# New tables of units, turns and product order in a two-layer trunk with seven-product weight pairs

## The chip, the cores and the metric

The kernel runs on one core of a Trainium2 chip. The metric is the device time of one execution in microseconds, the median of several runs. The profile is of one execution; its times are in microseconds from the start of its span.

## The reference

The reference is a trunk of two transformer layers in float32 on a sequence of 256 tokens with D = 2048, 16 heads of 128 and an MLP of 8192. What matters here is its chain of matrix products:

```python
u = rms_norm(h, a_norm_g[l]);  proj = u @ a_w_in[l]          # 2048 x 6160
o = forgetting_attention(q, k, v, logf)
h = h + o.reshape(B, S, D) @ a_w_out[l]
h = h + sq_relu_mlp(h, mlp_norm_g[0], mlp_w1[0], mlp_w2[0])  # a = relu(u @ w1); (a * a) @ w2
kv = rms_norm(h, kv_norm_g) @ kv_w
q = rms_norm(h, b_norm_g[l]) @ b_w_q[l]
o = chunked_relbias_attention(q, k_sh, v_sh, b_rel[l])
h = h + o.reshape(B, S, D) @ b_w_out[l]
h = h + sq_relu_mlp(h, mlp_norm_g[1], mlp_w1[1], mlp_w2[1])
```

All weights are used once and together are about 0.5 GB, so they stream through the core while TensorE works.

## The kernel before

**A unit.** A weight panel of 512 columns is read in units of two k-tiles, 128 x 1024 float32 numbers, 512 KB. `load` issues a unit's transfer on SP's queue into one of four buffers (`raw`). `issue` splits a unit in two: ScalarE copies it to `hi` (L256), VectorE computes `lo = raw - hi` (L257). TensorE then runs three passes (L519, L521, L523): activations' `hi` by `hi`, activations' `lo` by `hi`, activations' `hi` by `lo`. A whole unit is twelve matmuls of 512 columns. `top_up` keeps two split units ready ahead of the one that TensorE works on, and three units loaded beyond these. `hi` and `lo` have three buffers each.

**A pair.** In the MLPs and in the query projection two neighbouring panels, a and b, are a `Pair`. A part of its k-tiles goes through a seven-product scheme on 2 x 2 blocks (two halves of these k-tiles by two panels), with two blocks of tokens as the third side. Blocks are named 11, 12, 21, 22. Seven "made" forms are multiplied, in the order 11, T3, T2, T1, 21, T4, 22, where T3 = 22 + 12, T2 = T3 + 11, T1 = 12 + 11 and T4 = 21 + T2. In the MLPs all pairs but the first have eight k-tiles in the scheme (`deep`): a block is 128 x 2048, 1 MB, and a form is multiplied in two halves f and h of six matmuls each. The other eight k-tiles of each panel are its own units, a4 to a7 and b4 to b7. (The first pair and the query's two have four k-tiles in the scheme and own units from 2 on.)

**Where made forms come from.** `bring` loads blocks on SP's queue (L860) into four rooms of one buffer each, so the transfer waits until the room's last reader is done. The rooms change hands from pair to pair: block 12 goes where the pair before had 11, 22 where it had 12, 11 where it had 21, 21 where it had 22. T3 and T2 are sums on VectorE (L876) in a room of their own; T2 is made when T3 has been split. T1 and T4 are made by a transfer with addition (`put`, L882), issued from POOL: T1 adds block 11 onto the tile of 12, T4 adds block 21 onto the tile of T2, and that is issued when T2 has been split.

**The order of work.** `plan_mlp` writes one list of all items for a layer's MLP. W1 and W2 alternate: W2 of chunk c and W1 of chunk c + 1, each with q = 0 and 1. The orders of a cycle are called "deep0" (W2, q = 0), "ahead0" (W1, q = 0), "deep1" (W2, q = 1), "ahead1" (W1, q = 1). `Pair.plan` puts the first four forms in front, with b5, b6, b7 of the pair before between them, and then follows `ORDERS`, where each F stands for the next made form:

```python
plan = made[0] + rest[:1] + made[1] + rest[1:2] + made[2] + rest[2:] + made[3]
```

**When blocks are fetched.** After each own unit `prepare` looks at how many own units remain until the next pair starts, and issues what that pair's row of `UNITS` asks for at this count: loads of 12, 22, 21 and 11, the sum T3 (in two halves, the second a unit later) and the transfer for T1, in this order of the six numbers. A larger number is earlier. W1E belongs to the first pair, W1I1 to the second, W1F and W1S to W1 with q = 0 and 1, W2F, W2S and W2L to W2 with q = 0, with q = 1 and to the last one, QF and QS to the query's pairs.

**Small work.** Everything else is cut into steps in the queue `fill`; one step is run after each own unit and after each form of a deep pair. `TURNS` has the steps of a hidden panel (first row group: chunk 0, second: the later chunks; four panels each): the first number is the step of its transposing transfers (a `hop` of 16 transfers, half on SP and half on POOL, where the second number is -1, else a way through memory that needs a second step), then follow ReLU, the square's `hi`, the square, its `lo`, and for the first two panels the sums that the scheme needs of the activations. `LONG` and `SHORT` are the same for the panels of the residual stream.

**Queues.** VectorE, ScalarE, TensorE and SP execute in the written order (`keep_order`). SP issues unit loads, block loads, turns and half of the hops; an issue that waits for its room holds all that are behind it.

Of the kernel before, what the change touches and what calls it, by code (L numbers as in the profile page):

```python
# [26 lines left out]
NEG = -1.0e30  # L27
UN = 1024
AHEAD = 2
ORDERS = {  # L30
# [7 lines left out]
}  # L38
UNITS = {
    "W1I1": (9, 7, 6, 5, 4, 1),  # L40
    "W1F": (6, 5, 1, 4, 4, 1),
    "W1S": (6, 5, 2, 4, 4, 3),
    "W2F": (7, 5, 1, 5, 4, 3),
    "W2S": (8, 8, 3, 4, 3, 2),
    "W2L": (6, 6, 1, 3, 3, 1),
    "QF": (5, 4, 1, 4, 3, 3),
    "QS": (7, 5, 1, 4, 3, 2),
}
TURNS = (
    ((1, -1, 4, 5, 6, 6, 6, 9, 9),  # L50
     (0, -1, 3, 5, 7, 7, 8, 9, 9),
     (1, -1, 5, 7, 7, 7),
     (1, -1, 3, 4, 5, 5)),
    ((0, -1, 4, 14, 14, 14, 14, 19, 19),
     (0, 3, 7, 10, 10, 13, 16, 18, 19),
     (1, -1, 4, 6, 7, 7),
     (0, -1, 4, 5, 5, 5)),
)
EARLY = 3
# [3 lines left out]
DEEP = 2 * UN  # L63
WIDE1 = (1, 2, 3, 4, 5, 6, 7)
# [15 lines left out]
def trunk(ctx: ExitStack, tc: tile.TileContext, xT, xr, gs, hg, bf, wgate, w_in, w_oa, w1a, w1fa, w1sa, w2fa, w2sa,  # L80
# [68 lines left out]
    class Pair:  # L149
# [12 lines left out]
        def plan(self, rest):  # L162
            made = [self.items(f"f{i} h{i}" if self.wide else f"f{i}") for i in range(7)]
            own = ORDERS[self.order].split()
            plan = made[0] + rest[:1] + made[1] + rest[1:2] + made[2] + rest[2:] + made[3]
            n = 4
            for i in own:
                if i == "F":
                    plan += made[n]
                    n += 1  # L170
                else:
                    plan += self.items(i)
            return plan, self.items("b5 b6 b7")

    def plan_mlp(w1, w1f, w1s, w2f, w2s, tail, more=None):
        pairs = []

        def add(w, wf, ws, i, wides, order, when, cols=WIDE):
            j = wides.index(i) if i in wides else i - sum(1 for k in wides if k < i)
            names = ("11", "12", "21", "22")  # L180
            if i in wides:
                m = 8 - cols // 512
                src = [[None] * (8 - m) + [ws[m * (2 * j + q) + u] for u in range(m)] for q in range(2)]
                big = {k: wf[4 * j + m] for m, k in enumerate(names)}
            else:
                src = [[w[16 * j + 8 * q + u] for u in range(8)] for q in range(2)]
                big = {k: src[int(k[1]) - 1][int(k[0]) - 1] for k in names}
            pairs.append(Pair(big, src, order, len(pairs) % 2 == 0, when, cols if i in wides else UN))

        rooms = {"12": "v0", "22": "k0", "11": "k1", "21": "v1"}  # L190
        seq = [(0, 0, 0), (0, 0, 1)]
        for c in range(NCH):
            seq += [(1, c, 0)] + [(0, c + 1, 0)] * (c + 1 < NCH) + [(1, c, 1)] + [(0, c + 1, 1)] * (c + 1 < NCH)
        for m, (second, c, q) in enumerate(seq):
            i = 2 * c + q
            if second:
                add(None, w2f, w2s, i, WIDE2, "deep%d" % q, UNITS["W2L" if i == 7 else "W2S" if q else "W2F"], DEEP)
            else:
                add(w1, w1f, w1s, i, WIDE1, "ahead%d" % q if i else "early", (25, 20, 9, 15, 10, 8) if not i else UNITS["W1I1" if i == 1 else "W1S" if q else "W1F"], DEEP)
            pairs[-1].at = second, c, q  # L200
        if more is not None:
            for q in range(2):
                add(more, None, None, q, (), "" if q else "query", UNITS["QS" if q else "QF"])
                pairs[-1].at = 1, NCH, q
        plan, rest = [], [(tail, 0, u) for u in range(KT // UA - 3, KT // UA)]
        for p in pairs:
            p.rooms = rooms
            if p.adds:
                rooms = {"12": rooms["11"], "22": rooms["12"], "11": rooms["21"], "21": rooms["22"]}
            mine, rest = p.plan(rest)  # L210
            plan += mine
        plan += rest
        units.extend(Form(p, i, q == 3) if q > 1 else p.src[q][i] for p, q, i in plan)
        return plan

# [3 lines left out]
    queue(w_oa, n_out)  # L219
    tail_a = Tail(w_oa, n_out - 5)  # L220
    plan_a = plan_mlp(w1a, w1fa, w1sa, w2fa, w2sa, tail_a, w_qb)
    for i in range(w_kv.shape[0]):
        units.append(w_kv[i])
    queue(w_ob, n_out)
    tail_b = Tail(w_ob, n_out - 5)
    plan_b = plan_mlp(w1b, w1fb, w1sb, w2fb, w2sb, tail_b)
    ready = deque()

# [38 lines left out]
    def half_next():  # L267
        u = raws[0][0] if raws else units[0]
        return isinstance(u, Form) and u.half and not u.pair.deep

    def top_up(ahead=AHEAD, early=EARLY):
        while (units or raws) and sum(1 for r in ready if not r[2]) <= ahead and not (half_next() and any(r[2] for r in ready)):
            issue()
        while units and sum(1 for r in raws if r[1]) < early:
            load()

    def fetch(ahead=AHEAD, early=EARLY):
        top_up(ahead, early)
        return ready.popleft()[:2]
# [58 lines left out]
    def room(tag, name, dtype=F32):  # L338
        return qkv.tile([P, DEEP], dtype, name=name, tag=tag, bufs=1)
# [69 lines left out]
        return query[0][:, i * UN : i * UN + UN]  # L409


    LONG = ((0, 0, 1, 3, 10, 11, 12, 13, 13), (0, 1, 2, 4, 8, 9), (0, 1, 1, 3, 5, 6), (0, 0, 1, 3, 5, 6))
    SHORT = ((3, 1, 2, 3, 6, 7, 9, 9, 10), (4, 2, 3, 5, 10, 11, 13, 14, 22), (1, 2, 3, 4, 9, 10), (0, 0, 1, 2, 4, 5))

    def next_x(n, r2, stats, which, into, kept=None, fs=None, then=None, thirds=True):
        add_h = residual(n, r2)
        zt, way = [], []
        fs = fs if n < 1 + thirds else None
        at = (LONG if kept is not None else SHORT)[n]

# [41 lines left out]
    class RowStats:  # L462
# [4 lines left out]
        def add(self, b, n):  # L467
            t = wk.tile([P, 512], F32, name="sqr", tag="wk")
            S.activation(t, h[b][:, n * 512 : (n + 1) * 512], AF.Square, accum_out=self.ss[:, b * NG + n : b * NG + n + 1])
# [57 lines left out]
    def products(ps, hi, lo, x, u, halves=False, fast=None, apart=False):  # L527
        kw = {"skip_group_check": True} if fast else {}

        def item(j, b):  # L530
            k = u * UA + j if fast is None or u > 1 else 2 * j + u
            return ps[b], [x[k][:, i, b * P : (b + 1) * P] for i in range(2)], j, k == 0 and not fast, k == KT - 1

        J, B = range(UA), range(NB)
        if apart:
            groups = [[(j, b) for b in B] for j in J]
        elif halves:
            groups = [[(j, b) for j in J] for b in B]
        else:
            groups = [[(j, b) for b in B for j in J]]  # L540
        for g in groups:
            items = [item(*i) for i in g]
            for c in HALVES if halves and g is groups[-1] else (slice(0, 512),):
                passes(items, hi, lo, c, **kw)
# [14 lines left out]
    def panels(x, evacs, before=None, after=None, which=(None, None), tail=None):  # L559
        ps = [acc_pair(i) for i in which[: len(evacs)]]  # L560
        for u in range(KT // UA - (3 if tail else 0)):
            if before:
                before(u)
            for q, evac in enumerate(evacs):
                hi, lo = fetch(min(u // 2, AHEAD), 2) if before else fetch()
                products(ps[q], hi, lo, x, u, not units and not ready, apart=u < 2 if before else len(evacs) == 2 and (u, q) == (KT // UA - 1, 0))
# [196 lines left out]
    early = room("bias", "early")  # L763
# [120 lines left out]
    def prepare(p, d):  # L884
        if p.deep and d == p.units[4] - 1:
            make(p, "T3", 1)
        for name, at in zip(("12", "22", "21", "11", "T3", "T1"), p.units):
            if d == at and p.deep and name == "T3":
                make(p, "T3", 0)
            elif d == at:  # L890
                (bring if name[0] != "T" else put if p.adds and name == "T1" else make)(p, name)

    def mlp(plan, x, Sx, st, last, more=None):
        base = turns[0]
        hids = [[] for _ in range(NCH)]
# [57 lines left out]
        for i, (p, q, u) in enumerate(plan):  # L953
# [5 lines left out]
            if q > 1:  # L959
# [6 lines left out]
                if q == 2 + p.wide:  # L966
                    if not p.deep:
                        top_up(AHEAD - 1)
                    if u == 1:
# [170 lines left out]
```

## Time and profile before

| | us |
|---|---|
| median of 3 runs | 2092.68 (2088.75 to 2097.32) |
| the profiled execution | 2090.07 |
| its span | 2088.3 |
| TensorE busy | 2068.8 |
| VectorE busy | 1710.9 |
| ScalarE busy | 1313.2 |
| POOL busy | 224.7 |

The granted TensorE clock is 0.998 on average. The transfers move 543 MB, 260 GB/s on average. Lines of the profile name the engine, the kernel's line, the operation, the tile written and the tiles read; a bracket after it, or the part behind a bar, is the engine's idle time ahead of it and what ended that. A line of waits has the waiting instruction, whom it waited for, the total in us, the number of times and the longest. A line of a stretch (from:to) has its length, the busy time of PE, PE's weight loads, VectorE, ScalarE and POOL with the number of instructions, then TensorE's granted clock, the share of the transfer engines and GB/s. A line of transfers ends with their count, size and median time from issue to landing in us.

### The profile page before, as it was taken

The numbers are of one execution on the slowest core, as the hardware profiler recorded it, in microseconds if no ns is written. First come the engines' busy times: TensorE is split into PE (matmuls) and PEld (weight loads), VectorE is DVE, ScalarE is ACT, GpSimd is POOL, SyncE is SP. The second block draws the span as 40 slices with busy tenths as digits, with TensorE's granted clock in tenths as the row PEclk, the third lists the DMA queues.
The fourth block names the chain that finished last, engine by engine and source line by source line (L and its number), as shares of the span: only waits on it lengthen the run. The fifth ranks groups of instructions, "written<-read, shape, count | busy, mean of one in ns | idle before, by whom it ended". The sixth has DMA issues, their size and how long they took to land.

```text
span 2088.3 us, 26874 instructions
## 1 busy us (share of the span) xinstructions
PE 2068.8 (99%) x9140; PEld 1703.1 (82%) x9140; DVE 1710.9 (82%) x1974; ACT 1313.2 (63%) x1587; POOL 224.7 (11%) x339
## 2 busy tenths in 40 slices
PE   9999999999999999999999999999999999999999
PEld 7888888877888887888878888888788888888887
DVE  5767666898898898888988677768988988988986
ACT  6544444676676676576777445456766676766764
POOL 1111000021101102101011000000211111011020
PEclk9999999999999999999999999999999999999999
DMA  8777778787988898898978767787889889888875
GB/s 286 248 250 245 227 255 264 270 250 243 293 268 268 267 292 244 270 280 265 283 241 269 236 225 237 235 268 272 275 268 295 241 268 291 266 269 267 291 241 182
DMA packets 170682, 543.08 MB, mean 260 GB/s; under 512 B 40480, under 2 KB 68528, under 8 KB 147504
## 3 DMA queue, kind: packets, MB, share of 16 engines
q1 hardware_dynamic: 153008, 463.16, 62.9%
q0 software_dynamic: 17248, 77.64, 18.7%
q8 instruction: 72, 1.18, 0.2%
q10 hardware_dynamic: 288, 0.57, 0.1%
q14 instruction: 66, 0.54, 0.1%
HBM read 501.39 MB, written 26.24 MB: 253 GB/s over the span
## 4 chain that ended last, share of the span: by engine, by line
PE 76%; issue 10%; DMA 10%; DVE 3%; ACT 1%; POOL 0%; SPq 0%; ACTq 0%; DVEq 0%; POOLq 0%
PE acc L523 21%; PE acc L519 20%; PE acc L521 20%; PE s L523 4%; PE s L519 4%; PE s L521 4%; DVE lo L257 2%; DMA w<-in_w2fa 1%; DMA wT<-in_w2fa 1%; DMA turn<-z 1%; DMA wT<-in_w2fb 1%; ACT hi L256 1%; DMA w<-in_w2fb 1%; DMA w<-in_w1fb 1%; DMA raw<-in_w2sa 1%
## 5 line engine op out<-in xcount | busy, mean ns | idle before, releaser
L256 ACT ACTIVATE hi<-raw 128x1024 fp32r<-128x1024 f32 (+1 forms) x514 | 540.4, 1054 | 344.6 <-PE acc L521 257.6
L257 DVE TENSOR_TENSOR lo<-raw,hi 128x1024 fp32r<-128x1024 f32 (+1 forms) x514 | 618.6, 1212 | 165.0 <-ACT hi L256 150.0
L519 PE MATMUL acc<-hi,act 128*128 128x512 f32 x2076 | 580.7, 395 | 9.8 <-ACT hi L256 8.4
L523 PE MATMUL acc<-lo,act 128*128 128x512 f32 x2076 | 570.9, 390 | 1.0 <-DVE lo L257 0.6
L521 PE MATMUL acc<-hi,act 128*128 128x512 f32 x2076 | 570.4, 390 | 0.2
L519 PEld LDWEIGHTS acc<-hi,act 128*128 128x128 f32 x2076 | 387.6, 188 | 92.3 <-ACT hi L256 11.7
L523 PEld LDWEIGHTS acc<-lo,act 128*128 128x128 f32 x2076 | 389.0, 188 | 86.6 <-DVE lo L257 6.2
L521 PEld LDWEIGHTS acc<-hi,act 128*128 128x128 f32 x2076 | 390.2, 188 | 83.4 <-DVE act L350 1.5
L256 ACT ACTIVATE hi<-w 128x1024 fp32r<-128x1024 f32 x258 | 270.7, 1057 | 109.0 <-PE acc L521 68.2
L257 DVE TENSOR_TENSOR lo<-w,hi 128x1024 fp32r<-128x1024 f32 x258 | 310.1, 1219 | 18.9 <-ACT hi L256 17.7
L257 DVE TENSOR_TENSOR lo<-wT,hi 128x1024 fp32r<-128x1024 f32 x184 | 222.2, 1221 | 74.9 <-ACT hi L256 73.6
L256 ACT ACTIVATE hi<-wT 128x1024 fp32r<-128x1024 f32 x184 | 192.9, 1058 | 110.6 <-PE acc L521 35.6
L395 POOL DMA_DIRECT2D q<-z x208 | 105.6, 547 | 266.5 <-DVE z L369 127.2
L519 PE MATMUL s<-hi,act 128*128 128x512 f32 x358 | 98.5, 390 | 0.5 <-DVE s L976 0.5
L523 PE MATMUL s<-lo,act 128*128 128x512 f32 x358 | 98.5, 390 | 0.0
L521 PE MATMUL s<-hi,act 128*128 128x512 f32 x358 | 98.2, 389 | 0.0
L876 DVE TENSOR_TENSOR wT<-w,w 128x1024 f32<-128x1024 f32 x62 | 75.4, 1217 | 7.9 <-DMA w<-in_w1fb 2.7
L519 PEld LDWEIGHTS s<-hi,act 128*128 128x128 f32 x358 | 67.1, 188 | 14.8 <-issue 0.9
L523 PEld LDWEIGHTS s<-lo,act 128*128 128x128 f32 x358 | 67.0, 188 | 14.5 <-DVE lo L257 0.8
L521 PEld LDWEIGHTS s<-hi,act 128*128 128x128 f32 x358 | 67.2, 188 | 14.0
L876 DVE TENSOR_TENSOR wT<-wT,w 128x1024 f32<-128x1024 f32 x62 | 76.0, 1225 | 2.1
L605 POOL TENSOR_TENSOR ss<-ss,mhalf 128x4 f32<-128x4 f32 x32 | 43.3, 1360 | 273.0 <-DVE ss L604 272.8
(181 smaller groups left out, 1820.5 us busy)
## 6 DMA issues: line engine op xcount, KB each, us to landing
raw<-in_w_in SPq DMA_DIRECT2D x95, 512.0 KB, 4.3
w<-in_w2fa SPq DMA_DIRECT2D x32, 1024.0 KB, 6.7
raw<-in_w2sa SPq DMA_DIRECT2D x64, 512.0 KB, 6.5
raw<-in_w_kv SPq DMA_DIRECT2D x64, 512.0 KB, 4.5
w<-in_w2fb SPq DMA_DIRECT2D x32, 1024.0 KB, 6.5
raw<-in_w2sb SPq DMA_DIRECT2D x64, 512.0 KB, 6.6
w<-in_w1fa SPq DMA_DIRECT2D x28, 1024.0 KB, 7.7
raw<-in_w1sa SPq DMA_DIRECT2D x56, 512.0 KB, 7.1
```

The source lines that it names most:

```text
L256: S.activation(hi[:, c], raw[:, c], AF.Copy)
L257: V.tensor_tensor(lo[:, c], raw[:, c], hi[:, c].bitcast(F32), op=ALU.subtract)
L395: (G if i % 2 else SY).dma_start(dst[32 * j : 32 * j + 32, i * n : (i + 1) * n], z[32 * i : 32 * i + 32, j * n : (j + 1) * n])
L519: TE.matmul(ps[:, cols], xh, cut(hi, j), start=first, stop=False, **kw)
L521: TE.matmul(ps[:, cols], xl, cut(hi, j), start=False, stop=False, **kw)
L523: TE.matmul(ps[:, cols], xh, cut(lo, j), start=False, stop=last, **kw)
L605: G.tensor_tensor(rn, vv, mhalf, op=ALU.pow)
L876: V.tensor_tensor(d, a, b, op=ALU.add)
```

## The change

The change touches tables alone, and one new table `LAST`, by which an order may multiply its last three made forms in another sequence. In "deep0" that sequence is 21, 22, T4, and all three stand right behind a4. In "deep1" the last form moves behind a5. In "ahead1" T4 moves ahead of a5. The rows of `UNITS`, `TURNS`, `LONG` and `SHORT` get other numbers; the row of the first pair moves from the code into the table as W1E.

```diff
+LAST = {"deep0": (4, 6, 5)}
 ORDERS = {
...
-    "deep0": "a4 F F b4 a5 F a6 a7",
-    "deep1": "a4 F b4 F F a5 a6 a7",
+    "deep0": "a4 F F F b4 a5 a6 a7",
+    "deep1": "a4 F b4 F a5 F a6 a7",
     "ahead0": "F a4 F a5 a6 a7 F b4",
-    "ahead1": "a4 F a5 F a6 a7 F b4",
+    "ahead1": "a4 F F a5 a6 a7 F b4",
 }
 UNITS = {
-    "W1I1": (9, 7, 6, 5, 4, 1),
-    "W1F": (6, 5, 1, 4, 4, 1),
-    "W1S": (6, 5, 2, 4, 4, 3),
-    "W2F": (7, 5, 1, 5, 4, 3),
-    "W2S": (8, 8, 3, 4, 3, 2),
-    "W2L": (6, 6, 1, 3, 3, 1),
-    "QF": (5, 4, 1, 4, 3, 3),
-    "QS": (7, 5, 1, 4, 3, 2),
+    "W1E": (25, 20, 9, 14, 11, 10),
+    "W1I1": (9, 7, 5, 6, 4, 1),
+    "W1F": (7, 5, 1, 5, 4, 3),
+    "W1S": (8, 6, 4, 5, 4, 1),
+    "W2F": (6, 5, 1, 5, 4, 3),
+    "W2S": (7, 7, 4, 5, 3, 1),
+    "W2L": (7, 5, 1, 5, 4, 2),
+    "QF": (7, 6, 1, 3, 2, 1),
+    "QS": (7, 5, 1, 5, 2, 2),
 }
 TURNS = (
-    ((1, -1, 4, 5, 6, 6, 6, 9, 9),
-     (0, -1, 3, 5, 7, 7, 8, 9, 9),
-     (1, -1, 5, 7, 7, 7),
+    ((0, -1, 4, 5, 6, 6, 6, 7, 9),
+     (0, -1, 3, 6, 7, 7, 7, 8, 8),
+     (0, -1, 4, 7, 7, 7),
      (1, -1, 3, 4, 5, 5)),
-    ((0, -1, 4, 14, 14, 14, 14, 19, 19),
-     (0, 3, 7, 10, 10, 13, 16, 18, 19),
-     (1, -1, 4, 6, 7, 7),
+    ((1, -1, 5, 14, 14, 14, 15, 20, 20),
+     (0, 2, 8, 10, 10, 14, 18, 20, 22),
+     (0, -1, 5, 6, 7, 7),
      (0, -1, 4, 5, 5, 5)),
 )
...
             own = ORDERS[self.order].split()
+            last = LAST.get(self.order, (4, 5, 6))
...
-                    plan += made[n]
+                    plan += made[last[n - 4]]
...
-    ... "early", (25, 20, 9, 15, 10, 8) if not i else UNITS[...]
+    ... "early", UNITS["W1E" if not i else ...]
...
-    LONG = ((0, 0, 1, 3, 10, 11, 12, 13, 13), (0, 1, 2, 4, 8, 9), (0, 1, 1, 3, 5, 6), (0, 0, 1, 3, 5, 6))
-    SHORT = ((3, 1, 2, 3, 6, 7, 9, 9, 10), (4, 2, 3, 5, 10, 11, 13, 14, 22), (1, 2, 3, 4, 9, 10), (0, 0, 1, 2, 4, 5))
+    LONG = ((1, 0, 2, 4, 9, 11, 11, 13, 14), (0, 1, 2, 4, 7, 9), (0, 1, 1, 3, 5, 5), (0, 0, 1, 1, 4, 5))
+    SHORT = ((4, 1, 2, 3, 6, 6, 9, 9, 10), (4, 2, 3, 5, 10, 11, 13, 15, 23), (1, 2, 2, 3, 9, 9), (1, 0, 1, 2, 4, 5))
```

More of the change, by code (lines that the diff above doesn't have):

```diff
@@ L198, in plan_mlp @@
             else:
-                add(w1, w1f, w1s, i, WIDE1, "ahead%d" % q if i else "early", (25, 20, 9, 15, 10, 8) if not i else UNITS["W1I1" if i == 1 else "W1S" if q else "W1F"], DEEP)
+                add(w1, w1f, w1s, i, WIDE1, "ahead%d" % q if i else "early", UNITS["W1E" if not i else "W1I1" if i == 1 else "W1S" if q else "W1F"], DEEP)
             pairs[-1].at = second, c, q
```

## The prediction

> **What bounds the kernel now.** I read the totals of the page first, then TensorE's own waits.
>
> ```profile
> span 2088.3 us, 26874 instructions
> PE 2068.8 (99%) x9140; PEld 1703.1 (82%) x9140; DVE 1710.9 (82%) x1974; ACT 1313.2 (63%) x1587; POOL 224.7 (11%) x339
> ...
> PE acc L519 <- ACT hi L256: 8.4, 7, 2.6
> PE s L523 <- DVE lo L257: 2.0, 4, 1.0
> ```
>
> TensorE is the bound: 2088.3 - 2068.8 = 19.5 us of the span are not its own. The change adds and removes no matmul, so it can only move waits. In the timeline, a unit and a form at full pace, in the first pair of W1 that has the wide form, look like this:
>
> ```profile
> 442.84 1.07 PE L519 MATMUL acc<-hi,act 128*128 128x512 f32 x4
> 443.75 1.07 PE L521 MATMUL acc<-hi,act 128*128 128x512 f32 x4
> ...
> 445.56 0.62 PE L519 MATMUL acc<-hi,act 128*128 128x512 f32 x2
> ```
>
> Four matmuls take 443.75 - 442.84 = 0.91 us, 0.2275 us each, and a unit of twelve takes 445.56 - 442.84 = 2.72 us. A form is six and six, so one step of a plan, unit or form, is 2.72 us. The busy time of PE hides short waits (ends are modelled), so I count starts. In stretches of 8 us:
>
> ```profile
> 480.00:488.00 8.00, 6.13 (x28) 4.73 (x26) 4.40 (x5) 1.98 (x3) 3.94 (x8) 1.00 0.79 205
> 488.00:496.00 8.00, 7.54 (x26) 6.06 (x27) 6.89 (x6) 7.38 (x9) 0.03 (x1) 0.79 0.87 294
> 648.00:656.00 8.00, 7.28 (x31) 5.37 (x29) 5.87 (x8) 3.57 (x5) 3.95 (x8) 1.00 0.75 192
> 816.00:824.00 8.00, 6.63 (x29) 4.85 (x28) 5.29 (x6) 3.87 (x4) 2.77 (x6) 1.00 0.73 203
> 980.00:988.00 8.00, 8.00 (x37) 6.64 (x36) 7.69 (x8) 4.92 (x6) 3.89 (x8) 1.00 0.86 281
> 1519.00:1527.00 8.00, 8.00 (x37) 6.52 (x36) 6.91 (x7) 4.80 (x6) 3.97 (x8) 1.00 0.84 239
> 1684.00:1692.00 8.00, 7.94 (x34) 5.96 (x33) 6.60 (x7) 5.00 (x6) 3.00 (x7) 1.00 0.81 256
> 1848.00:1856.00 8.00, 7.45 (x31) 5.50 (x31) 6.09 (x7) 3.86 (x4) 3.87 (x8) 1.00 0.70 199
> 2013.00:2021.00 8.00, 7.94 (x35) 6.08 (x35) 6.87 (x8) 4.64 (x5) 3.40 (x7) 1.00 0.80 269
> ```
>
> The first bracket counts matmuls. An undisturbed stretch has 37, as the rows at 980 and 1519 show. These nine rows lie around the eight places where a "deep0" pair (W2, q = 0) comes to its form T4. They lack 9, 11, 6, 8, 0, 0, 3, 6 and 2 matmuls, 45 in all, and 45 x 0.2275 = 10.2 us. That is nearly half of all that TensorE loses in the MLPs: sixteen further stretches that I looked at lack 55 (12.5 us), these six among them:
>
> ```profile
> 445.00:453.00 8.00, 7.23 (x31) 5.34 (x30) 6.63 (x8) 6.73 (x8) 0.00 (x0) 1.00 0.96 386
> 573.00:581.00 8.00, 7.78 (x35) 6.12 (x34) 6.36 (x7) 5.05 (x6) 0.00 (x0) 1.00 1.04 333
> 738.00:746.00 8.00, 7.02 (x31) 5.51 (x30) 6.41 (x6) 5.82 (x6) 0.00 (x0) 1.00 0.96 301
> 1076.00:1084.00 8.00, 6.77 (x29) 4.96 (x28) 4.06 (x5) 4.07 (x7) 0.68 (x1) 1.00 0.98 358
> ...
> 1754.00:1762.00 8.00, 7.64 (x33) 5.69 (x32) 4.68 (x5) 6.44 (x8) 0.92 (x1) 1.00 0.86 299
> 1937.00:1945.00 8.00, 7.93 (x35) 6.27 (x34) 5.91 (x6) 5.58 (x6) 0.00 (x0) 1.00 0.95 309
> ```
>
> **What ends the wait in deep0.** The chain, the timeline and the table of waits agree:
>
> ```profile
> 473.85 13.40 DMA wT<-in_w2fa
> ...
> 487.36 2.00 ACT L256 ACTIVATE hi<-wT 128x1024 fp32r<-128x1024 f32 x2 [6.02 <-DMA wT<-in_w2fa]
> 488.46 0.99 PE L519 MATMUL acc<-hi,act 128*128 128x512 f32 x2 [2.34 <-ACT hi L256]
> ...
> ACT hi L256 <- DMA wT<-in_w2fa: 19.7, 6, 6.0
> ```
>
> T4 is made by a transfer that adds block 21 onto T2. It is issued as soon as T2 has been split, takes 13.40 us here, and then ScalarE copies, VectorE subtracts and TensorE starts. Between T2 and T4 in deep0 lie b7, T1, a4 and 21. That is about one step too little.
>
> The row at 488 also shows a granted clock of 0.79 after this one wait; the two stretches around it lack 20 matmuls, 4.6 us, though the idle time is 2.34 us. [...]
>
> **Part by part.**
>
> *deep0: "a4 F F F b4" with made order 21, 22, T4.* T4 comes one step (2.72 us) later after T2, and 22, a raw block that is there long before, fills in. Seven of the eight waits are shorter than 2.72 us; the first is about as long. All but some 0.4 us of the 10.2 go: -9.8 us. The room of T4 comes free a step later; it is the next pair's T3, which is made at b4, and b4 itself moves behind T4, so nothing queues there.
>
> *ahead1: "a4 F F a5" instead of "a4 F a5 F".* The same thing the other way round: T4 comes 2.72 us earlier. How much room it had:
>
> ```profile
> 442.88 2.01 ACT L256 ACTIVATE hi<-wT 128x1024 fp32r<-128x1024 f32 x2 [2.41 <-DMA wT<-in_w1fa]
> ...
> 611.77 2.15 ACT L256 ACTIVATE hi<-wT 128x1024 fp32r<-128x1024 f32 x2 [1.02 <-DMA wT<-in_w1fa]
> 613.12 1.07 PE L519 MATMUL acc<-hi,act 128*128 128x512 f32 x4
> ...
> 1481.98 2.01 ACT L256 ACTIVATE hi<-wT 128x1024 fp32r<-128x1024 f32 x2 [2.56 <-PE acc L523]
> 1484.51 0.62 PE L519 MATMUL acc<-hi,act 128*128 128x512 f32 x2
> ...
> wT<-in_w2fa POOLq DMA_DIRECT2D x8, 1024.0 KB, 10.6
> wT<-in_w1fa POOLq DMA_DIRECT2D x7, 1024.0 KB, 9.3
> ```
>
> A copy is half of the row at 442.88, about 1.05 us. In the pair at 611.77 it is done at 612.8, and T4's matmuls would be wanted at 613.12 (where a5 stands now): just in time, with VectorE's part, about 1.2 us more against 0.91 us of matmuls, a tenth too late. At 442.88 the copy ends at 443.9, wanted at 442.84: 1.1 us late, with VectorE's part 1.4. At 1481.98 it ends at 1483.0, wanted at 1484.51 - 2.72 = 1481.79: 1.2 late, 1.6 with the rest. The six others are like the one at 611.77 or a little looser: 0.5 us together. Sum +3.5 us. Bounds: nothing, if the transfers of the first pair meet less traffic; 10.2 us, if these T4 behave as deep0's do now. I take 3.5, because the median landing, 9.3, is that of W1, not the 10.6 of W2.
>
> *deep1: form 22 moves behind a5, and W1S loads 22 at 6 instead of 5.* At 738, 573 and 1937 deep1 waits in front of 22:
>
> ```profile
> 741.95 1.23 DVE L876 TENSOR_TENSOR wT<-w,w 128x1024 f32<-128x1024 f32 x1 [0.82 <-DMA w<-in_w1fa]
> 743.10 2.35 DVE L257 TENSOR_TENSOR lo<-w,hi 128x1024 fp32r<-128x1024 f32 x2
> ```
>
> The sum T3 of the next pair waits for its load, and the subtraction for 22 stands behind it on VectorE. The load comes a unit earlier and 22 a unit later: 6 + 2 + 2 matmuls, -2.3 us. The first load of that row, 12, goes from 6 to 8, but it needs the room of block 11, which is only free when T2 is made: it holds SP's queue for that time. Units are loaded three ahead, 8.2 us, which covers it: 0.
>
> *Hidden turns: ReLU at step 5 instead of 4 in the later chunks, sums spread to 20 and 22.* The wait at 1754 (4 matmuls) stands behind a ReLU whose turned tile is still landing:
>
> ```profile
> ACT q L899 <- DMA q<-z: 5.4, 4, 2.0
> ```
>
> One step later takes it out: -0.9 us.
>
> *T1 of deep1 (W2S, 2 to 1).* It may now stand behind the eight turn transfers on POOL:
>
> ```profile
> 648.96 3.55 POOL L395 DMA_DIRECT2D q<-z  x7 [5.41 <-DVE z L369]
> ...
> w<-in_w2fa POOLq DMA_DIRECT2D x8, 1024.0 KB, 9.3
> ```
>
> Eight by 0.51 are 4.1 us, 9.3 to land, 1.05 to copy: 14.5 us, and from b4 to T1 lie six steps, 16.3 us. The steps hide it; without a margin of 1.8 us it would cost its excess six times.
>
> *All else* (W1E, W1I1, W2F, W2L, QF, QS, LONG, SHORT) has one answer, no term of its own: loads asked for a unit earlier or later mostly wait for their room, not for the table. The wait at 1076 is a turned tile of the last panel on its way, which LONG doesn't shorten. But some sixty numbers are new, and each can put two bursts together. The other sixteen places cost 12.5 us with the old numbers; 3.2 of it are counted as gone above. New ones are bounded by nothing and by another 12.5; I take about a quarter, +3.5 us.
>
> **Sum:** -9.8 + 3.5 - 2.3 - 0.9 + 3.5 = -6.0 us. The profiled execution took 2090.07 us, 1.8 more than its span, so it would take 2084.1. It lies 2.6 below the median of 2092.68; from the median, 2086.7 us, 0.29% less.
>
> **Rivals.**
>
> *All waits go.* ahead1's T4 is in time everywhere and the new tables make no new waits, even take 1 us off the rest: -9.8 - 2.3 - 0.9 - 1.0 = -14.0, 2078.7 us. For it: every edit that I can price, except ahead1, loosens a wait that the trace shows. Against it: the rows at 442.88 and 1481.98 say that two T4 are late.
>
> *The wait only moves from deep0 to ahead1.* T4 in ahead1 then costs the full 10.2: -13.0 + 10.2 + 3.5 = +0.7, 2093.4 us. For it: after the change ahead1 has the order, and the load of 12 at 6, which deep0 has now. Against it: 12 waits for T2 in either place, and W1's landings are shorter. [...]
>
> *Slower: SP's queue stands.* In deep1 the load of 21 now comes at b4 and waits until the split of 22, which has moved behind a5. Behind it stand all unit loads of b5 and on, and the turns' transfers. From b4 to 22 are three steps, 8.2 us, and the units loaded ahead cover as much. If the hold outlasts them, TensorE waits for the excess, and with a slow clock for more. At 3.5 us in each of the six deep1 pairs before a W1: -9.5 + 3.5 + 21.0 = +15, 2107.7 us. It decides against the change from an excess of 1.0 us (six times that eat the 6.0), and passes 0.5% from 2.8 us. Against it: SP runs ahead of TensorE, so the hold begins and ends early.
>
> **How the numbers follow.** Forecast 0.52, all waits go 0.18, moves 0.17, slower 0.13. About 0.5% (10.5 us) is what a measurement of this kernel can tell from no change: 2082.2 and 2103.1 are the marks. Faster: the 0.18 and the lower edge of the forecast, 0.07, together 0.25. Slower: nearly all of the 0.13 and a little of the moved wait, 0.13. Same: 0.62. The range runs from 2077, below the case in which all goes, to 2102: it leaves out the slower case and the extremes of the others. Its upper part takes in ahead1's bound of 10.2 and new waits of up to 12.5 us together: -13.0 + 10.2 + 12.5 = +9.7, 2102.4.
>
> **What would show it.** Right: in deep0 T4's copy no longer ends a wait on "DMA wT<-in_w2f", counts of 36 or 37 there; in ahead1 a first copy that waits for "DMA wT<-in_w1f", with 1 to 2 us of PE idle in the first wide W1 pair of each layer and next to nothing later; no VectorE wait for "w<-in_w1f" ahead of T3 in deep1. Wrong: PE idle over 1 us in the later ahead1 pairs, waits on "raw<-in_w2s" in deep1, or a second stretch with a granted clock below 1.

## The result, and the profile after

| | before | after |
|---|---|---|
| median of 6 runs, us | 2090.91 (2088.75 to 2097.32) | 2077.85 (2074.23 to 2080.62) |
| the profiled execution, us | 2090.07 | 2078.09 |
| its span, us | 2088.3 | 2076.2 |
| TensorE's waits in the pairs, us | 23.0 | 13.4 |

The ratio is 0.9932, with an interval of 0.9916 to 0.9949. The forecast was 0.29% less, and it became 0.68%, more than twice as much. The time lies just inside the lower end of the range (2077 to 2102), beside the rival "all waits go" (2078.7 us).

The last row of the table is used throughout. It is worked out from the starts of the 8838 matmuls of the three passes: whatever the distance from one start to the next has beyond 0.232 us is summed over the pairs of the MLPs and of the query projection. It counts waits and slow matmuls alike, and does not suffer from modelled ends.

The page of the kernel after, its totals and the head of its chain:

```profile
span 2076.2 us, 26893 instructions
...
PE 2062.0 (99%) x9140; PEld 1702.9 (82%) x9140; DVE 1712.5 (82%) x1974; ACT 1313.2 (63%) x1587; POOL 222.9 (11%) x339
...
PE 95%; DMA 3%; ACT 1%; DVE 1%; issue 0%; POOL 0%; ACTq 0%; DVEq 0%; SPq 0%; POOLq 0%
```

The other engines' busy times are within 2 us of those of before, as it must be where nothing but the order changes. PE's busy time is 6.8 us shorter; I read that as short waits and slow matmuls that the busy time had hidden. The span minus it is 14.2 us, where it was 19.5.

The stretches around deep0's T4, in the kernel after (columns as in the prediction; the first bracket counts TensorE's matmuls, 37 is a full stretch):

```profile
478.00:486.00 8.00, 8.00 (x37) 6.64 (x36) 7.15 (x9) 4.87 (x6) 3.97 (x8) 1.00 0.67 174
648.00:656.00 8.00, 8.00 (x37) 6.60 (x36) 7.46 (x8) 6.05 (x7) 1.22 (x3) 1.00 0.79 277
812.00:820.00 8.00, 8.00 (x37) 6.60 (x36) 7.46 (x7) 6.58 (x7) 0.54 (x2) 1.00 0.78 280
1518.00:1526.00 8.00, 7.75 (x35) 6.10 (x34) 4.99 (x6) 6.12 (x7) 0.00 (x0) 1.00 0.83 328
1840.00:1848.00 8.00, 8.00 (x37) 6.64 (x36) 7.49 (x7) 6.06 (x7) 1.81 (x4) 1.00 0.70 237
2003.00:2011.00 8.00, 8.00 (x37) 6.64 (x36) 7.60 (x8) 6.06 (x6) 2.02 (x5) 1.00 0.71 242
```

Five of the six rows are full, where the nine rows of before lacked 45; the granted clock is 1.00 in all. The row at 1518 lacks two, not at T4 but at b4, the unit behind it: there the ReLU of a hidden turn waits 1.62 us on ScalarE for its turned tile, and b4's copy stands behind it. T4 of deep0 no longer stops TensorE. What still does, in the table of waits of the kernel after (waiting instruction, whom it waited for, total in us, number, longest):

```profile
PE acc L522 <- ACT hi L259: 3.4, 3, 1.3
PE s L522 <- ACT hi L259: 2.6, 2, 2.4
...
ACT hi L259 <- DMA wT<-in_w1fa: 9.3, 5, 3.1
...
ACT hi L259 <- DMA raw<-in_w2sa: 6.7, 4, 4.8
```

All lines are three higher than before (L256 is L259, L519 is L522, L860 is L863). The first row was 8.4 us in seven waits. The transfer that TensorE is kept waiting for at T4 is now W1's, in ahead1, no longer W2's. ScalarE still waits for W2's in four places, 5.7 us together, which costs TensorE nothing. And there is a wait that before did not have: a plain unit of W2 (`raw<-in_w2sa`), which TensorE meets as the 2.4 of the second row.

By place, the 23.0 us went as follows:

| place | before | after |
|---|---|---|
| T4 in deep0 and b4 right behind it (8 pairs; after, all of it at b4) | 9.4 | 0.7 |
| form 22 in deep1 | 2.05 | 0 |
| T4 in ahead1, first wide W1 pair of each layer | 0 | 3.3 |
| first wide pairs: a6, T3, 11 | 4.5 | 1.6 |
| T2 in deep1, second layer | 0.9 | 0 |
| last W2 pairs | 1.2 | 0 |
| query pairs | 3.15 | 2.9 |
| own unit b5 in deep1 | 0 | 2.65 |
| the rest | 1.8 | 2.2 |

Of the 12.1 us between the spans 1.9 lie ahead of the first item of the pairs: it starts at 375.6 us in the trace of before and at 373.7 after. That is not put down to the change, although `SHORT` and W1E do move a little ahead of that item. In the seventeen traces of this study it starts either between 373.1 and 374.1 or between 375.1 and 375.7, with either tables: the kernel after showed 373.7, 375.6 and 373.7, and the old `SHORT` and the old loads of W1E showed 375.6 in the kernel before and 373.9 in the kernel with deep0's order alone.

### The profile page after: what moved, and what is told of

It reads as the page before. It is cut to its first block, busy times and chain, and to the rows that moved or that the text cites. A ratio compares the mean times of both kernels' runs of the same rounds, so it can differ in the third digit from the quotient of the medians.

```text
span 2076.2 us, 26893 instructions
## 1 busy us (share of the span) xinstructions
PE 2062.0 (99%) x9140; PEld 1702.9 (82%) x9140; DVE 1712.5 (82%) x1974; ACT 1313.2 (63%) x1587; POOL 222.9 (11%) x339
## 4 chain that ended last, share of the span: by engine, by line
PE 95%; DMA 3%; ACT 1%; DVE 1%; issue 0%; POOL 0%; ACTq 0%; DVEq 0%; SPq 0%; POOLq 0%
PE acc L526 25%; PE acc L524 25%; PE acc L522 25%; PE s L522 6%; PE s L524 6%; PE s L526 6%; PE s L666 1%; PE po L696 1%; DMA raw<-in_w2sa 1%; DMA wT<-in_w1fa 1%; DMA raw<-in_w2sb 1%; DMA raw<-in_w1b 0%; DMA query<-turn 0%; ACT hi L259 0%; PE po L697 0%; PE s L665 0%
## 5 line engine op out<-in xcount | busy, mean ns | idle before, releaser
L259 ACT ACTIVATE hi<-raw 128x1024 fp32r<-128x1024 f32 (+1 forms) x514 | 540.4, 1054 | 341.4 <-PE acc L524 251.4
L522 PE MATMUL acc<-hi,act 128*128 128x512 f32 x2076 | 578.3, 394 | 5.4 <-ACT hi L259 3.4
L522 PEld LDWEIGHTS acc<-hi,act 128*128 128x128 f32 x2076 | 387.4, 188 | 85.4 <-ACT hi L259 4.5
L259 ACT ACTIVATE hi<-w 128x1024 fp32r<-128x1024 f32 x258 | 271.1, 1058 | 120.9 <-PE acc L524 105.5
L259 ACT ACTIVATE hi<-wT 128x1024 fp32r<-128x1024 f32 x184 | 193.3, 1059 | 88.6 <-PE acc L524 34.6
L522 PE MATMUL s<-hi,act 128*128 128x512 f32 x358 | 98.8, 391 | 3.1 <-ACT hi L259 2.6
L522 PEld LDWEIGHTS s<-hi,act 128*128 128x128 f32 x358 | 66.8, 188 | 18.4 <-ACT hi L259 3.9
```

Source lines behind the costliest of these rows:

```text
L259: S.activation(hi[:, c], raw[:, c], AF.Copy)
L522: TE.matmul(ps[:, cols], xh, cut(hi, j), start=first, stop=False, **kw)
```

## The experiments

The first four kernels were to decide between two theories: A, the order of deep0 was the bulk, as the prediction had it; B, the order helps only together with the new tables. A third, theory C of the later texts, came after these four: much of the gain is the steps', because a ReLU had stood in front of a copy that T4's transfer waits for. Below, "waits" are TensorE's in the pairs of the profiled execution, counted as above; ratios are against the kernel before on the same chip, with their interval.

| kernel | ratio | waits, us |
|---|---|---|
| orders alone | 1.0001 [0.9985, 1.0018] | 30.3 |
| deep0's order alone | 0.9987 [0.9973, 1.0001] | 25.9 |
| UNITS alone | 1.0016 [1.0000, 1.0032] | 31.8 |
| steps alone (TURNS, LONG, SHORT) | 0.9953 [0.9938, 0.9969] | 18.1 |
| three step numbers | 0.9938 [0.9922, 0.9954] | 14.7 |
| deep0's order and W2L | 0.9932 [0.9918, 0.9946] | 16.0 |
| the same and the three step numbers | 0.9924 [0.9908, 0.9940] | 12.9 |
| after, steps undone | 1.0015 [0.9996, 1.0033] | 31.7 |
| after, deep0's order undone | 0.9958 [0.9944, 0.9972] | 14.4 |
| after, second time | 0.9918 [0.9899, 0.9938] | 19.4 |
| after, third time | 0.9926 [0.9911, 0.9941] | 9.1 |

**One part alone.** Four kernels are the kernel before with one part of the change each. Orders alone:

```diff
+LAST = {"deep0": (4, 6, 5)}
-    "deep0": "a4 F F b4 a5 F a6 a7",   "deep1": "a4 F b4 F F a5 a6 a7",   "ahead1": "a4 F a5 F a6 a7 F b4",
+    "deep0": "a4 F F F b4 a5 a6 a7",   "deep1": "a4 F b4 F a5 F a6 a7",   "ahead1": "a4 F F a5 a6 a7 F b4",
```

> The kernel before with all three new orders, its units, steps and residual tables unchanged. Theory A: deep0 -8.7, ahead1's T4 +3.3 to +6 (its room shrinks by one step of 2.72 us and the old steps put sums on VectorE there), deep1's wait in front of 22 -2: 4 to 7 us faster. Theory B: at most 2 us faster, or slower.

Nothing is gained (1.0001). T4 of deep0 is in time, but T4 of ahead1 is late in all eight pairs, by 0.7 to 2.1 us, 8.6 us together. That is the prediction's rival "the wait only moves". It is not all: the last W2 pair of each layer waits, 7.4 us together, where it was 0.3, for a reason that the next kernel shows.

deep0's order alone, the lines LAST and "deep0" of this diff:

> The kernel before with the new deep0 order (21, 22, T4 behind a4) and nothing else. Theory A (deep0's T4 was the bulk): the eight T4 waits of deep0, 9.4 us by the spacing of the matmuls, shrink to under 1 us, everything else stays: 8 to 9 us faster than before, some 2082 us. Theory B (the order only helps together with the new tables, since the load of 12 at 6 still falls into T4's transfer): the waits shrink by less than half, under 4 us faster.

The waits on T4 of deep0 are gone here, as the prediction said, and still the time is nearly that of before. Its timeline in the last W2 pair of the first layer, and its table of waits:

```profile
987.17 0.90 SPq L863 DMA_DIRECT2D w<-in_w2fa  x2
...
995.48 2.01 ACT L259 ACTIVATE hi<-w 128x1024 fp32r<-128x1024 f32 x2 [6.98 <-DMA w<-in_w2fa]
...
996.59 0.73 PE L522 MATMUL acc<-hi,act 128*128 128x512 f32 x2 [2.80 <-ACT hi L259]
```

```profile
PE acc L522 <- ACT hi L259: 7.2, 3, 2.8
...
ACT hi L259 <- DMA w<-in_w2fb: 9.7, 3, 6.8
```

Block 11 of the last W2 pair is asked for at the fourth number of W2L, 3, which is after a5. In the old order form 22 still lies between a5 and the next pair, in the new one only a6 and a7 do, so the same number leaves the load a step less. It is issued at 987.17, lands 8.2 us later, and TensorE stands 2.80 us; in the trace of before it is issued at 989.80 and TensorE comes to it at 1001.59. The two last pairs cost 5.8 and 4.4 us. I had put W2L under "no term of its own". It is the other half of the order.

UNITS alone, all rows of the diff with W1E to QS:

> The kernel before with the new table of units alone. Theory A: the T4 waits of deep0 stay at 6 to 10 us (they depend on the place of T4, and the load of 12 at 7 takes a little traffic out of its transfer): 0 to 4 us faster. Theory B (loads at other times shorten T4's transfer itself): at least 7 us faster, and the transfer of deep0's T4 under 9.8 us in the median.

No gain either: T4 of deep0 still waits in seven of the eight pairs, by 0.75 to 1.8 us.

TURNS, LONG and SHORT alone:

> The kernel before with the new TURNS, LONG and SHORT alone. Theory A: the places where ScalarE or VectorE stood in a burst go: first wide pair and the form behind it, 4.5 us to some 2, the ReLU behind a landing turn, 0.9 to 0, the last W2 pair, 1.2 to 0: 3 to 5 us faster, and deep0's T4 waits unchanged. Theory B: no difference over 2 us, because these places only become free when the orders change.

This one is the surprise. Without touching an order it takes 0.47% off, and of deep0's eight waits on T4 three are left, 4.45 us where there were 9.4.

**Which step.** In the trace of before, ScalarE and VectorE in a deep0 pair around the second half of T2, on which TensorE starts at 641.68:

```profile
638.43 0.58 ACT L970 ACTIVATE s<-s 128x512 f32<-128x512 f32 x1
639.03 1.06 ACT L899 ACTIVATE q<-q 128x1024 f32<-128x1024 f32 x1
640.00 1.04 ACT L256 ACTIVATE hi<-wT 128x1024 fp32r<-128x1024 f32 x1
...
641.07 1.23 DVE L257 TENSOR_TENSOR lo<-wT,hi 128x1024 fp32r<-128x1024 f32 x1 [2.28 <-ACT hi L256]
```

The ReLU of a hidden turn (L899) stands ahead of the copy of T2. T2 is split at 641.07 + 1.23 = 642.30, 0.62 us after TensorE has started on its `hi`. TensorE does not wait here, since it needs `lo` only four matmuls later. But T4's transfer is issued when T2 has been split, so the pair starts it late. In the trace of before this is so in six of the eight deep0 pairs, by 0.6 us; in the first of each layer T2 is split 0.2 us ahead of TensorE's start. Two ReLUs and the last sums of panel 0 (two entries) make up what is called the three step numbers here; in the kernel before they are moved alone:

```diff
-    ((0, -1, 4, 14, 14, 14, 14, 19, 19),    # later chunks, panel 0
+    ((0, -1, 5, 14, 14, 14, 14, 20, 20),
-     (1, -1, 4, 6, 7, 7),                    # panel 2
+     (1, -1, 5, 6, 7, 7),
```

> The kernel before with three numbers of the later chunks' TURNS changed: the ReLU of panels 0 and 2 at step 5 instead of 4, the last sums of panel 0 at 20 instead of 19. That takes ScalarE's 1.05 us of small work out of the step of form T3, ahead of the split of T2. Theory C (the steps give most of the gain, because they bring T2's split, and with it the transfer of T4, about 1.07 us earlier in every deep pair after the first): deep0's T4 waits fall from 9.4 us to 4 or 5, the 0.9 us ahead of T2 in layer B goes, 5 to 6.5 us faster than before. Theory D (the 0.47% of all the new steps come from the first chunk, LONG and SHORT): under 2 us faster, T4's waits as before.

The same place in its timeline:

```profile
635.55 0.58 ACT L970 ACTIVATE s<-s 128x512 f32<-128x512 f32 x1
636.05 1.05 ACT L256 ACTIVATE hi<-wT 128x1024 fp32r<-128x1024 f32 x1
637.00 1.05 ACT L899 ACTIVATE q<-q 128x1024 f32<-128x1024 f32 x1
...
637.13 1.23 DVE L257 TENSOR_TENSOR lo<-wT,hi 128x1024 fp32r<-128x1024 f32 x1 [1.21 <-ACT hi L256]
```

The subtraction stands 637.13 - 635.55 = 1.58 us behind the row L970, where it was 2.64: 1.06 us earlier, one ReLU. The ReLU now takes its turn after the copy. The three numbers bring 0.62%; the sums among them were not tried apart from the ReLUs. T4 of deep0 waits 3.9 us instead of 9.4. Of these 5.5 us 2.5 are in the six later pairs (5.3 to 2.8), and 3.0 in the first pair of the first layer, which the numbers do not touch: T2 is split 0.2 us ahead there in both traces, and T4's transfer took 11.7 us from issue to landing instead of 13.4. The table of waits has:

```profile
PE acc L519 <- ACT hi L256: 4.1, 5, 2.0
...
ACT hi L256 <- DMA wT<-in_w2fa: 15.4, 5, 4.2
```

**deep0's order with the row that it needs.** The kernel before with LAST, the "deep0" line and

```diff
-    "W2L": (6, 6, 1, 3, 3, 1),
+    "W2L": (7, 5, 1, 5, 4, 2),
```

> The kernel before with the new deep0 order and the new row W2L (11 at 5 instead of 3, sums at 4 and 3, T1 at 2), nothing else. Theory C: with the order alone the last W2 pair waited for its block 11, 5.8 us in layer A and 4.4 in layer B, which ate what T4 gave; with the row these waits go: 8 to 11 us faster than before. Theory D (deep0's new order costs in other places as well): at most 4 us faster.

0.9932: with block 11 asked for two units earlier (at 5 instead of 3; the row's other loads move by one) the wait of the last W2 pair is gone and the order brings what it promised. So each of two mechanisms alone, this one and the three step numbers, brings over 0.6%. Together:

> The new deep0 order, the new row W2L and the three numbers of TURNS together, all else of before. Theory C: T4's waits and those of the last W2 pair are gone, T2's is gone: MLP waits of 12 to 14 us instead of 23, 9 to 12 us faster than before, as far as the whole change brings it (the two parts overlap in T4's waits, so it is less than their sum). Theory D: no better than the better one of the two.

0.9924, not 0.987. Both loosen the same wait, one by 2.72 us and the other by 1.06, and what is gone cannot go twice. It lies among the three ratios of the whole change (0.9932, 0.9918, 0.9926), and the intervals overlap. So these two parts bring as much as all of it, as far as the runs can tell; the remaining orders and rows show no gain of their own.

**Undoing one part of the change.** The kernel after with the old TURNS, LONG and SHORT:

> The changed kernel with the old TURNS, LONG and SHORT: new orders and units alone. Theory C: T2's split is 1.07 us late again in the deep0, deep1 and ahead1 pairs, deep0's T4 bears it, but ahead1's T4, which has 0.4 to 1.2 us of room in the changed kernel, doesn't: its waits are 0.3 to 1 us in each of the eight pairs, and the first pairs lose some 2 us: 5 to 9 us slower than the changed kernel (0.995 to 0.997 of before). Theory G (orders and units have their own room): within 2 us of the changed kernel.

All is lost (1.0015). Its stretches at two places of the first layer, and its waits:

```profile
608.00:616.00 8.00, 5.94 (x20) 4.41 (x19) 6.17 (x9) 5.18 (x7) 0.00 (x0) 0.79 0.75 311
924.00:932.00 8.00, 5.48 (x24) 4.21 (x24) 5.61 (x7) 5.90 (x7) 0.00 (x0) 1.00 0.83 264
```

```profile
PE acc L522 <- ACT hi L259: 12.8, 9, 2.1
PE s L522 <- ACT hi L259: 7.6, 4, 3.6
...
ACT hi L259 <- DMA wT<-in_w1fa: 22.6, 7, 5.7
...
ACT hi L259 <- DMA raw<-in_w2sa: 18.2, 7, 6.0
```

T4 of ahead1 is late in all eight pairs, 16.9 us together, and b5 of deep1 in four, 10.2 us. Here both rivals, "the wait only moves" and "SP's queue stands", are what happens. It is the steps that keep ahead1's T4 in time in the six pairs after the first of each layer: there T2 is split 0.3 to 0.5 us ahead of TensorE's start in the kernel after, and 0.6 to 0.9 behind it with the old steps. Their transfers also take longer here, 10.6 to 12.3 us from issue to landing, where the kernel after has 9.7 to 10.8. In the first pair of each layer T2 is split 0.2 us ahead with either steps, and T4 is 1.6 to 1.8 us late in either kernel. Whether the steps also act on b5 this trace does not show, since b5's waits change from execution to execution (below).

The kernel after with deep0's old order, LAST empty:

> The changed kernel with the old deep0 order (T4 right behind 21). Theory C (the step tables took half of deep0's T4 waits by themselves, the order the rest): T4 of deep0 waits 3 to 6 us in all, 3 to 6 us slower than the changed kernel. Theory H (with the new steps and loads the order is without effect): under 1 us of T4 waits, no difference.

0.9958 where the whole change, run for the third time on the same chip, has 0.9926. The order is worth some 0.3% on top of the rest. T4 of deep0 waits again, 5.0 us in the starts; its table of waits:

```profile
PE acc L522 <- ACT hi L259: 6.0, 5, 1.7
...
ACT hi L259 <- DMA wT<-in_w2fa: 16.2, 5, 3.8
```

**The new wait at b5.** In the kernel after, SP's queue and what it led to, from the timeline of the first deep1 pair:

```profile
563.84 0.47 SPq L242 DMA_DIRECT2D raw<-in_w2sa  x1
570.48 1.75 SPq L388 DMA_DIRECT2D q<-turn  x4
573.64 0.35 SPq L863 DMA_DIRECT2D w<-in_w1fa  x1
574.04 2.21 SPq L242 DMA_DIRECT2D raw<-in_w2sa  x3
...
586.59 1.06 ACT L259 ACTIVATE hi<-raw 128x1024 fp32r<-128x1024 f32 x1 [4.82 <-DMA raw<-in_w2sa]
...
587.70 1.19 PE L522 MATMUL s<-hi,act 128*128 128x512 f32 x4 [2.38 <-ACT hi L259]
```

The load of block 21 (573.64) is issued 0.02 us after the split of 22, whose room it takes (the subtraction for it is done at 573.62). The three unit loads at 574.04 stand behind it and go out together; b5's lands 12.4 us later, and TensorE stands 2.65 us by its starts. This is the rival "SP's queue stands", with a wait in one pair of six instead of in all. If the hold is its cause, asking for 21 two units later removes it:

```diff
-    "W1S": (8, 6, 4, 5, 4, 1),
+    "W1S": (8, 6, 2, 5, 4, 1),
```

> The changed kernel with one number put back: W1S loads 21 at 2 instead of 4, so that SP's queue no longer stands until the split of 22 with the unit b5 behind it. Theory E (that hold is the cause of the waits for b5 in deep1, 2.65 us in one execution and 4.09 and 4.10 in another): no wait for a unit of W2 at b5 over 0.3 us, MLP waits 11 to 14 us, 1 to 6 us faster than the changed kernel (0.989 to 0.992 of before). Theory F (the transfers were merely crowded in these stretches): such waits are there again, at b5 or elsewhere.

Ratio 0.9903 [0.9885, 0.9921], waits 8.5 us, and none at b5. The same with the old order of ahead1 in all pairs, or in the first wide W1 pair alone, where its T4 is late:

> The changed kernel with W1S's 21 at 2 and the old ahead1 order in all pairs. T4 of ahead1 then has 3 to 4 us of room everywhere. Theory E: like the kernel with the first pair alone, within 1 us, since the later ahead1 pairs don't wait in the changed kernel. If ahead1's new order was needed for other reasons (the sum T3 of the next pair), new waits at T3 or 11 of the deep0 pairs, 2 us or more.

> The changed kernel with W1S's 21 at 2 and the old ahead1 order in the first wide pair of W1 alone, where T4 came 1.6 and 1.75 us late. Theory E: both kinds of waits go, MLP waits 9 to 12 us, another 2 to 3 us faster than with 21 alone, if the burst that stood ahead of a6 there in the kernel before (1.3 and 0.8 us) doesn't return. If it returns, no gain over 21 alone.

0.9899 [0.9879, 0.9919] and 0.9907 [0.9890, 0.9925], no better than 0.9903; waits 14.2 (in the slowest of its six runs, 2080.81 us) and 11.1 us. T4's wait in the first pair goes, but the a6 of the same pair waits again (1.48 and 1.30 us with the old order in that pair alone). In all seventeen traces a6 waits there with the old order of ahead1, by 0.5 to 2.8 us, and not with the new one. The order of ahead1 is a wash there.

The kernel after twice more, and the one with 21 later once more:

> The changed kernel once more, for its waits in another execution and for a time on the same chip. If the one wait for a unit of W2 in layer A (2.65 us, behind the load of 21 on SP's queue) is the rule, it is there again; if it hung on a crowded moment, it is under 0.5 us. 12 to 15 us faster than before.

> The changed kernel a third time, beside the next one. Waits for b5 in deep1 between none and 9 us, as the moment has it; 0.991 to 0.994 of before.

> The changed kernel with W1S's 21 at 2, a second time. Theory E: again no wait for b5, MLP waits of 8 to 11 us, 0.989 to 0.991 of before, 2 to 6 us faster than the changed kernel on this chip. Theory F: no difference to it.

The waits on W2's units of the kernel after, second time:

```profile
PE s L522 <- ACT hi L259: 6.5, 3, 2.9
...
ACT hi L259 <- DMA raw<-in_w2sa: 14.8, 7, 5.5
```

and the third time:

```profile
PE s L522 <- ACT hi L259: 0.5, 1, 0.5
```

b5's wait comes and goes from execution to execution: 2.65 us in one pair, 4.09 and 4.10 in two, then 0.73. (The second time the profiled execution was the slowest of six, 2086.51 us, where the median is 2079.29.) In the four traces of kernels with 21 later there is none over 0.15 us. The hold alone does not make the wait, though. The five traces with 21 at 4 and the new order of deep1 (the kernel after three times, the one with old steps, the one with deep0's old order) have thirty such pairs. In every one b5's load is issued 0.4 us behind the split of 22. In the 21 without a wait it goes out 10.2 to 11.1 us ahead of TensorE's start on b5 and lands in 6.1 to 9.8 us; in the nine with a wait it takes 10.5 to 13.6. With 21 later, b5's load goes out 11.8 to 15.2 us ahead in all 24 pairs, and lands in 5.6 to 7.8. So in these traces a wait comes where the hold and a long landing meet. What makes the landing long stays open, and so does whether the hold has a part in that. The second ratio of the kernel with 21 later is 0.9922 [0.9908, 0.9937], beside 0.9926 [0.9911, 0.9941] for the kernel after on the same chip: that the later number makes the kernel faster is not shown.

## Where the prediction was right, and where it failed

The direction was right, and deep0's order did to its wait what it said. The size was not: 12.1 us between the two spans where -6.0 stood. In the sum the step that failed is "All else", +3.5 us: the places under it fell by 1.3. In the mechanism it is the ReLU's step, priced at -0.9 for the one wait that bore its name: the three step numbers alone bring 0.62%, and with all the new steps undone the whole change brings nothing. Of the rest of the difference, the other terms were 1.1 us too hopeful, 1.9 us lie ahead of the pairs and are luck of the execution, and some 0.5 lie elsewhere outside the pairs.

*deep0, -9.8.* The waits went as it said: 9.4 us became 0.7. But the order is not the only way to them: the three step numbers alone halve them in the six pairs that they act on. And it needed W2L, which had no term: alone, the order gave nearly all of its gain back, most of it in the last W2 pairs. Undone from the whole it costs 0.3%, about 7 us. Nothing queues at b4, the prediction said; but the 0.7 us that are left stand there, and in the second execution of the kernel after 1.5 us in one pair.

*ahead1, +3.5.* Predicted were 1.4 and 1.6 us in the first wide W1 pair of each layer and 0.5 in the others. They became 1.58 and 1.75, and next to nothing elsewhere. In the timeline of the kernel after:

```profile
440.77 0.73 PE L526 MATMUL acc<-lo,act 128*128 128x512 f32 x2
441.38 2.01 ACT L259 ACTIVATE hi<-wT 128x1024 fp32r<-128x1024 f32 x2 [1.13 <-DMA wT<-in_w1fa]
442.48 0.74 PE L522 MATMUL acc<-hi,act 128*128 128x512 f32 x2 [0.98 <-ACT hi L259]
```

Two matmuls from 440.77 take 0.455 us; the next start should be at 441.23 and is at 442.48. The term was right in size. For the six others that was partly luck: I had read them as just in time with T2 split late, and with the old steps they lose 13.6 us (the kernel with the steps undone). Nor did the transfer itself become shorter:

```profile
wT<-in_w2fa POOLq DMA_DIRECT2D x8, 1024.0 KB, 10.3
...
wT<-in_w1fa POOLq DMA_DIRECT2D x7, 1024.0 KB, 10.3
```

W1's row had 9.3 before. It mixes pairs of ahead0 and ahead1; the six later pairs of ahead1 alone, in both layers, took 8.9 to 9.9 before and 9.7 to 10.8 after, so that the 1.06 us by which they start earlier are nearly used up. My reason for 3.5 rather than 10.2, that W1's landing is shorter than W2's, did not hold: both rows have 10.3 now. The term also left out what this order takes away: the wait at a6 in the first wide pair, 2.1 us in the trace of before, goes with it.

*deep1's 22, -2.3.* 2.05 became 0: right.

*T1 of deep1, 0 with a margin of 1.8 us.* No wait appeared; in the six pairs ahead of a W1 the room shrank from 7.3 us or more to between 2.1 and 4.8.

*The ReLU's step, -0.9.* By place it came true, and yet its mechanism is the one that failed. I looked for a wait behind L899, found one of 0.9 us in a deep1 pair, which did go, and stopped. The ReLU's larger cost did not carry its name: it delayed ScalarE's next copy, the copy delayed VectorE, VectorE the issue of T4's transfer, and TensorE's wait was put down to that transfer more than 10 us later. Measured alone the three numbers bring 0.62%, some 13 us in time. From trace to trace the waits fall by 8.3 us (23.0 to 14.7) and the spans by 8.6; but the one trace of the kernel before is of 2090.07 us, and its median on the chip where the three numbers ran is 2097.69. What the traces tie to the ReLU is 2.5 us at T4 in the six later deep0 pairs and the 0.9 at T2; what the rest of the 13 us is they do not show. 0.9 it was not. In the sum this did not show, because deep0's order takes the same waits at T4, and because the earlier split of T2 is what let the term of ahead1 come true.

*All else, +3.5.* This failed in the sum. By the table, the places outside the four terms fell by 1.3 us, with the new wait of 2.65 at b5 in it: the bursts in the first wide pairs (2.9 us, 2.1 of them the a6 that ahead1's order takes away) and the waits in the last W2 pairs (1.2) went. So this term was 4.8 us too high. It was a quarter of 12.5 us, for "some sixty new numbers", and stood on no row. The sum by places, as the two traces have it, is -8.7 + 3.3 - 2.05 - 0.9 - 1.3 = -9.65 us where -6.0 stood.

*The rivals.* "All waits go" came closest in time (2078.7 against 2077.85 us), though its condition, ahead1 in time everywhere, was not met: 3.3 us stayed and others went. That it came so near is luck: it had not priced the places that went. The rival "moves" and the rival "SP's queue stands" are real, as the kernel with the old steps shows. The new steps hold off the first; that they hold off the second is not shown. The hold of SP ends with the split of 22, in every pair, some 11 us ahead of b5, and the waits of 0.73 to 4.10 us come where the load takes 10.5 us or more; I had argued that it begins and ends early.

*The clock.* In the pairs no stretch with a granted clock under 1 stayed in the profiled execution, as forecast. In the second execution of the kernel after there are two, 0.79 and 0.82 at their lowest (592 to 600 and 760 to 768 us), each behind a wait at b5. Waits on `raw<-in_w2s` in deep1 were named as a sign of being wrong, and they appeared.

## What to carry to other kernels

A wait that a slow transfer ends is not to be priced at the transfer alone: follow back what releases its issue, through each engine that works in the written order, for an instruction in front of the releasing copy (here a ReLU of 1.06 us) can be paid at the end, under another name. Parts that loosen the same wait do not add, and a part that only shifts work may need a number elsewhere (here W2L) before it brings anything; so price an order together with the loads that take its rooms. Many small numbers of unknown effect are not a positive term by themselves: look at what the moved steps stand in front of before guessing a sign.

## What the runs showed of the hardware

TensorE's pace after a wait did not hang on the length of the wait alone. In the seventeen traces nine waits in the pairs are longer than 2.2 us (start to start, less the usual distance). After those of 2.22, 2.50, 2.58, 3.05 and 3.73 us seven or eight matmuls followed at 0.427 us apart, about 1.6 us more; after 2.55, 2.68, 2.81 and 2.96 us none or one did. After the shorter ones none did. The 2.50 is the wait at 488.46 in the kernel before, where the granted clock was 0.59 from 488 to 492 us. The 2.55 is the wait at 587.70 in the kernel after, where it was 1.00 from 584 to 592 us. The 2.96 is the one at 996.59 with deep0's order alone: the two matmuls behind it take 0.57 us from start to start, 0.285 each. So 2.22 us was enough in one trace and 2.96 us was not in another; what decides it the traces do not show.

The time that an accumulating transfer of 1 MB takes from issue to landing is no constant of the kernel. W1's in the six later pairs of ahead1 took 8.9 to 9.9 us in the kernel before, 9.7 to 10.8 in the kernel after, and 10.6 to 12.3 in the kernel after with the old steps, where T2, which releases its issue, is split 1.0 to 1.4 us later against TensorE. Whether a load beside it lengthens it was not tried by itself.
